# Layer 2's first two weight blocks: the fourth quarter added by VectorE from a second load instead of by an accumulating DMA

## The chip, the cores and the metric

The kernel runs on one core of one Trainium2 chip. The metric is the device time of one execution in microseconds. Before the change it is 2123.89 us, the median of 3 runs (2120.89 to 2127.05). A profile of one more execution shows what each engine did: PE (matmuls), DVE (VectorE), ACT (ScalarE), POOL (GpSimd, here above all an issuer of DMAs) and SP (issues DMAs only).

## The reference

A two-layer encoder on 512 tokens of width 2048: a gated attention layer, then a gated retention layer, each followed by a residual layer norm. The change lies in the first product of the second layer:

```python
def retention_mixer(h, w_in, decay_exp, w_out, cos, sin):
    B, S, _ = h.shape
    proj = h @ w_in                     # 512 x 2048 times 2048 x 12288, float32
    q, k, v, g = jnp.split(proj, [R_QK_WIDTH, 2 * R_QK_WIDTH, 2 * R_QK_WIDTH + R_V_WIDTH], axis=-1)
    ...
    return (o * jax.nn.silu(g)) @ w_out
```

## The kernel before, in words

**Seven products for eight.** The columns of `w_in` are taken 1024 at a time, as twelve *blocks* (`r_in`, numbered from 0). A block is 2048 x 1024 and is cut into four quarters, B11, B12, B21 and B22, of 1024 x 512. The activations are cut likewise. Instead of eight quarter products the kernel makes seven, numbered 1 to 7, each of a *form* of the activations (a sum or difference of their quarters) and a sum of weight quarters. What each product needs of the weights, in the order of a block: 1 takes B11; 2 takes B21; 5 takes B11+B12; 6 takes B11+B12+B22; 3 takes B22; 7 takes B22+B12; 4 takes all four summed.

**Chunks.** A quarter comes as four *chunks* a to d of 128 x 1024 numbers (512 KB). 1/5b below is block 1, product 5, chunk b. Each chunk is split for PE into a high part `whi` (ACT casts it) and a low part `wlo` (DVE subtracts), both at L116, called hi and lo below. PE then makes 12 matmuls of it, three for each of four pairs (L263 with hi, L264 with lo, L265 with hi again), so the first matmul of a chunk needs its hi and the second its lo. There are three buffers for hi and three for lo: a chunk's hi can be written when PE is through with the chunk three before it.

**Order of the products.** PE's order is written by hand. For layer 2's first three blocks it interleaves them (`LAYER_SEQ`): 0/1, 0/2, 1/1, 1/2, 0/5, 0/6, 0/3, 0/7, 1/5, 0/4, 1/6, 1/3, 1/7, 2/1, 1/4, then the rest of block 2. Splits are made two chunks ahead of PE (`AHEAD`), loads are asked for three chunks ahead of a split (`FETCH`). The order on ACT, DVE, POOL and SP is made by a scheduler when the kernel is built; on each engine instructions run strictly in that order, so one that waits holds all behind it.

**Buffers and sums of weights.** Loads (`raw_load`, L126 and L127, from SP) go into the pool `rp`, 9 buffers of a chunk each, or, with `large`, into the pool `xp`, 32 buffers of the same size that hold the activations' quarters and forms. In blocks 0 and 1 (`first`) B11 is loaded again for product 5 and B12 is added to it by an accumulating DMA (`onto`, L144, issued by POOL). That buffer, `v`, then lives through the whole block: B22 is added to it by DVE for product 6 (L182), and when product 6 is split, POOL adds B21 onto it by DMA for product 4 (L203 and L204). B22 has four `rp` buffers of its own from product 6 to 7, and B12 is added onto them by DMA for product 7. In later blocks product 2 comes last but one, so its B21 still lies in SBUF and DVE adds it for product 4 (L183 and L184).

Of the kernel before, what the change touches and what calls it, by code (L numbers as in the profile page):

```python
# [29 lines left out]
R_G = R_HEADS // 2 * 3  # L30
# [22 lines left out]
def encoder_trunk_kernel(  # L53
# [19 lines left out]
    nc = tc.nc  # L73
# [13 lines left out]
    def nm(s):  # L87
        n_names[0] += 1
        return f"{s}{n_names[0]}"
# [4 lines left out]
    def x4(name, dt=F32R):  # L94
        return xp.tile([P, 1024], dt, tag="x", name=nm(name))
# [29 lines left out]
    def raw_load(src, large=False):  # L125
        raw = x4("raw", F32) if large else rp.tile([P, CH], F32, tag="raw", name=nm("raw"))  # L126
        x = nc.sync.dma_start(out=raw, in_=src)  # L127
        if fetched[0] < 12:
            in_turn(x)
        return raw  # L130

    def in_turn(x):

        tc.keep_in_program_order(x)
# [3 lines left out]
    def behind_split(x, n):  # L138

        tc.add_manual_dep(x.ins, los[-n].ins.name, mybir.DependencyInfo(  # L140
            mybir.DependencyClass.NoSync, mybir.DependencyReason.DATA), reason="behind_split")

    def onto(x, src):
        return nc.gpsimd.dma_start(out=x, in_=src, accum_op=ALU.add)  # L144

    class Block:


        def __init__(self, w, first, nc=4, hold=False):

            self.w, self.first, self.nc, self.hold = w, first, nc, hold
            self.got, self.keep, self.bk, self.hooks = {}, {}, {}, {}

        def add(self, seq):
# [7 lines left out]
        def fetch(self, p, c):  # L162
            q = lambda n: self.quarter(n, c)
            g = self.got
            if p == 1:
                g[1 if self.first else "v", c] = raw_load(q(11), self.hold)
            elif p == 2:
                g[2, c] = raw_load(q(21))
            elif p == 6:
                g[3, c] = raw_load(q(22))  # L170
            elif p == 5 and self.first:
                if self.hold:
                    g["v", c] = g[1, c]
                else:
                    g["v", c] = raw_load(q(11))
                    onto(g["v", c], q(12))

        def make(self, p, c):

            g, v = self.got, self.got.get(("v", c))  # L180
            if p == 6:
                nc.vector.tensor_add(v, v, g[3, c])  # L182
            elif p == 4 and not self.first:  # L183
                x = nc.vector.tensor_add(v, v, g[2, c])  # L184
                if self.nc == 4:
                    behind_split(x, 3)
            if p in (3, 7):
                return g[3, c]
            return g[p, c] if p == 2 or p == 1 and self.first else v
# [6 lines left out]
        def follow(self, p, c):  # L196
            q = lambda n: self.quarter(n, c)
            g = self.got
            if p == 1 and not self.first:
                onto(g["v", c], q(12))  # L200
            elif p == 3:
                onto(g[3, c], q(12))
            elif p == 6 and self.first:  # L203
                onto(g["v", c], q(21))  # L204

    class Plain:
# [310 lines left out]


    a_in = [Block(a["wa_in"][g], g < 2, hold=g == 0) for g in range(A_G)]
    r_in = [Block(a["wr_in"][g], g < 2) for g in range(R_G)]  # L520
    a_out = [Plain(a["wa_o"][g], A_KEEP if g == GROUPS - 1 else 4) for g in range(GROUPS)]
    r_pairs = [[Block(a["wr_p"][i, cg], False, 2) for cg in range(2)] for i in range(PAIRS)]
    r_out = [Plain(a["wr_o"][h], 4 - h * (4 - R_KEEP)) for h in range(2)]
# [696 lines left out]
```

## Time and profile before

| | |
|---|---|
| three timed runs | 2127.05, 2123.89, 2120.89 us |
| profiled execution, device time | 2125.48 us |
| its span, first to last instruction | 2123.4 us |
| granted PE clock, mean | 0.997 |
| PE, DVE, ACT, POOL busy | 2102.1, 1602.7, 1102.6, 368.0 us |
| PE waits for other engines, all | 10.4 us |

A row of a timeline gives the start and the duration in us from the span's start, the engine, the line, the operation, what is written and read, and in brackets the idle time of the engine just before, with what ended it. `raw<-raw,raw` at L182 is DVE's addition of B22, `wlo<-raw,whi` the lo of a chunk, `f<-xf,f` the lo of a form of the activations. A row of the windows gives, for a stretch, its length, the busy time of PE, of PE's weight loads, of DVE, ACT and POOL, each with a count, then the granted PE clock, the busy share of the DMA engines and GB/s.

### The profile page before, as it was taken

What the parts mean: (1) busy time and instruction counts of PE and PEld (TensorE: products, weight loads), DVE (VectorE), ACT (ScalarE), POOL (GpSimd) and SP (SyncE); (2) the same over time, 40 slices, a digit from 0 to 9 for tenths busy, and PEclk for the clock granted to TensorE, in tenths of its full rate; (3) what the DMA queues carried; (4) which work ended last, traced back from release to release, by engine and by line L of the source; (5) the groups of instructions that cost most, each with busy time, mean ns of one, the idle gap of its engine ahead of it and who ended that gap; (6) DMA issues with size and microseconds to landing.
All of it is one profiled execution on the core that took longest, in us unless ns stands there. A gap on an engine that the chain in (4) does not pass through costs nothing.

```text
span 2123.4 us, 26496 instructions
## 1 busy us (share of the span) xinstructions
PE 2102.1 (99%) x9756; PEld 1743.3 (82%) x9756; DVE 1602.7 (75%) x2198; ACT 1102.6 (52%) x1457; POOL 368.0 (17%) x453
## 2 busy tenths in 40 slices
PE   9999999999999999999999999999999999999997
PEld 7788888888888887888888888888888878888886
DVE  7778887977677886666877686666686887979767
ACT  6455556655543564454445444444456665656432
POOL 1242322000000112121111111111211122222200
PEclk9999999999999999999999999999999999999999
DMA  9866656563223587686686785576575578877862
GB/s 346 207 143 147 193 152 173 151 224 104 95 70 109 191 186 182 169 226 166 182 234 166 193 219 147 130 209 167 123 211 158 184 180 192 178 192 176 212 199 79
DMA packets 115057, 369.81 MB, mean 174 GB/s; under 512 B 14064, under 2 KB 17136, under 8 KB 114928
## 3 DMA queue, kind: packets, MB, share of 16 engines
q0 software_dynamic: 45568, 148.92, 33.8%
q1 hardware_dynamic: 68928, 218.29, 30.7%
q8 instruction: 76, 1.25, 0.2%
q10 hardware_dynamic: 432, 0.92, 0.1%
q14 instruction: 53, 0.43, 0.1%
HBM read 307.26 MB, written 60.82 MB: 173 GB/s over the span
## 4 chain that ended last, share of the span: by engine, by line
PE 88%; DVE 5%; DMA 4%; issue 2%; POOL 1%; ACT 0%; POOLq 0%; SPq 0%; DVEq 0%; ACTq 0%
PE acc L265 25%; PE acc L264 25%; PE acc L263 25%; PE tr L515 3%; PE o L263 2%; PE o L265 2%; PE o L264 2%; DMA raw<-in_wa_in_dram 1%; DVE wlo L116 1%; PE s L263 1%; PE s L265 1%; PE s L264 1%; DMA xf<-in_xq_dram 1%; DMA q<-qD 1%; DMA raw<-in_wr_p_dram 0%
## 5 line engine op out<-in xcount | busy, mean ns | idle before, releaser
L116 DVE TENSOR_TENSOR wlo<-raw,whi 128x1024 fp32r<-128x1024 f32 (+1 forms) x598 | 727.0, 1217 | 360.0 <-ACT whi L116 354.6
L116 ACT CAST whi<-raw 128x1024 fp32r<-128x1024 f32 (+1 forms) x598 | 626.0, 1050 | 656.9 <-PE acc L265 519.1
L263 PE MATMUL acc<-whi,f 128*128 128x512 f32 x2240 | 881.1, 393 | 3.1 <-ACT whi L116 3.1
L264 PE MATMUL acc<-wlo,f 128*128 128x512 f32 x2240 | 874.2, 390 | 4.0 <-DVE wlo L116 4.0
L265 PE MATMUL acc<-whi,f 128*128 128x512 f32 x2240 | 874.2, 390 | 0.0
L264 PEld LDWEIGHTS acc<-wlo,f 128*128 128x128 f32 x2240 | 421.7, 188 | 91.8 <-DVE wlo L116 6.6
L263 PEld LDWEIGHTS acc<-whi,f 128*128 128x128 f32 x2240 | 421.4, 188 | 89.0 <-ACT whi L116 4.2
L265 PEld LDWEIGHTS acc<-whi,f 128*128 128x128 f32 x2240 | 421.3, 188 | 88.6
L144 POOL DMA_DIRECT2D raw<-in_wr_in_dram x104 | 91.5, 880 | 389.8 <-DVE wlo L116 213.2
L263 PE MATMUL acc<-whi,ogh 128*128 128x512 f32 x288 | 115.6, 401 | 0.4 <-ACT ogh L116 0.4
L265 PE MATMUL acc<-whi,ogl 128*128 128x512 f32 x288 | 112.7, 391 | 0.0
L264 PE MATMUL acc<-wlo,ogh 128*128 128x512 f32 x288 | 112.5, 391 | 0.0
L182 DVE TENSOR_TENSOR raw<-raw,raw 128x1024 f32<-128x1024 f32 x80 | 97.5, 1220 | 8.8 <-DMA raw<-in_wr_in_dram 7.3
L379 ACT COPY t<-acc 128x512 f32<-128x512 f32 x138 | 78.7, 587 | 44.7 <-PE acc L265 40.4
L498 POOL TENSOR_TENSOR rstd<-rs_e,neg_half 128x1 f32<-128x1 f32 x40 | 30.4, 760 | 364.0 <-DVE rs_e L497 363.0
L184 DVE TENSOR_TENSOR raw<-raw,raw 128x1024 f32<-128x1024 f32 x64 | 77.7, 1214 | 0.0
L744 ACT ACTIVATE p<-s,nmax,q_rs 128x512 f32<-128x512 f32 x64 | 49.9, 779 | 33.1 <-DVE nmax L742 26.4
L116 DVE TENSOR_TENSOR f<-xf,f 128x1024 fp32r<-128x1024 f32 (+2 forms) x52 | 59.9, 1155 | 7.7 <-ACT f L116 7.6
L144 POOL DMA_DIRECT2D raw<-in_wa_in_dram x48 | 42.7, 890 | 126.1 <-DVE wlo L116 93.5
L265 PEld LDWEIGHTS acc<-whi,ogl 128*128 128x128 f32 x288 | 54.1, 188 | 12.1 <-DVE ogl L116 0.4
L263 PEld LDWEIGHTS acc<-whi,ogh 128*128 128x128 f32 x288 | 54.2, 188 | 10.2 <-ACT ogh L116 0.8
L264 PEld LDWEIGHTS acc<-wlo,ogh 128*128 128x128 f32 x288 | 54.3, 189 | 9.5
(183 smaller groups left out, 2365.2 us busy)
## 6 DMA issues: line engine op xcount, KB each, us to landing
raw<-in_wr_in_dram SPq DMA_DIRECT2D x152, 512.0 KB, 4.8
raw<-in_wr_in_dram POOLq DMA_DIRECT2D x104, 512.0 KB, 5.9
raw<-in_wa_in_dram SPq DMA_DIRECT2D x62, 512.0 KB, 5.5
raw<-in_wa_in_dram POOLq DMA_DIRECT2D x48, 512.0 KB, 8.4
raw<-in_wr_p_dram SPq DMA_DIRECT2D x36, 512.0 KB, 5.1
raw<-in_wa_o_dram SPq DMA_DIRECT2D x32, 512.0 KB, 3.6
raw<-in_wr_p_dram POOLq DMA_DIRECT2D x24, 512.0 KB, 7.2
yD<-t POOLq DMA_DIRECT2D x36, 256.0 KB, 7.2
```

What stands on the lines that cost most here:

```text
L116: x, y = nc.scalar.copy(hi, src), nc.vector.tensor_sub(lo, src, hi.bitcast(F32))
L144: return nc.gpsimd.dma_start(out=x, in_=src, accum_op=ALU.add)
L182: nc.vector.tensor_add(v, v, g[3, c])
L184: x = nc.vector.tensor_add(v, v, g[2, c])
L263: nc.tensor.matmul(ps, sh, mh, start=start, stop=False, skip_group_check=go_on)
L264: nc.tensor.matmul(ps, sh, ml, start=False, stop=False, skip_group_check=go_on)
L265: nc.tensor.matmul(ps, sl, mh, start=False, stop=stop, skip_group_check=go_on)
L379: nc.scalar.copy(keep[p, t], bk[CHAIN[p]][t])
L498: nc.gpsimd.tensor_tensor(out=dst, in0=e[:, :n], in1=neg_half[:, :n], op=ALU.pow)
L515: nc.tensor.transpose(out=b[:, tcols(i)], in_=src[:, tcols(i)], identity=ident)
L744: nc.scalar.activation(pt, sb, AF.Exp, scale=rs, bias=nmax, accum_out=self.sm[:, h:h + 1])
```

## The change

For layer 2's blocks 0 and 1 (`again`), the accumulating DMA of B21 after product 6 is left out. Instead B21 is loaded once more, from SP into `rp`, when product 4 is due, and DVE adds it to `v` before product 4's split; that addition may not be ordered before the lo of three chunks earlier (`behind_split`). For block 1 (`wide`) B22 comes into `xp` instead of `rp`.

```diff
@@ def fetch(self, p, c):
             elif p == 2:
                 g[2, c] = raw_load(q(21))
             elif p == 6:
-                g[3, c] = raw_load(q(22))
+                g[3, c] = raw_load(q(22), self.wide)
+            elif p == 4 and self.again:
+                g[2, c] = raw_load(q(21))
@@ def make(self, p, c):
-            elif p == 4 and not self.first:
+            elif p == 4 and (not self.first or self.again):
                 x = nc.vector.tensor_add(v, v, g[2, c])
                 if self.nc == 4:
                     behind_split(x, 3)
@@ def follow(self, p, c):
-            elif p == 6 and self.first:
+            elif p == 6 and self.first and not self.again:
                 onto(g["v", c], q(21))
@@
-    r_in = [Block(a["wr_in"][g], g < 2) for g in range(R_G)]
+    r_in = [Block(a["wr_in"][g], g < 2, again=g < 2, wide=g == 1) for g in range(R_G)]
```

Lines behind these are 3 lower in the new kernel (L182 becomes L185, L184 becomes L187). The order of PE's matmuls is the same in both. On SP, the order of the loads from product 1/5 on was, before:

```order
L127 DMA raw1398_7135<-in_wr_in_dram 128x1024
L127 DMA raw1401_7158<-in_wr_in_dram 128x1024
L127 DMA raw1406_7181<-in_wr_in_dram 128x1024
L127 DMA raw1409_7200<-in_wr_in_dram 128x1024
L127 DMA raw1424_7293<-in_wr_in_dram 128x1024
L127 DMA raw1429_7315<-in_wr_in_dram 128x1024
L127 DMA raw1432_7333<-in_wr_in_dram 128x1024
L127 DMA raw1435_7351<-in_wr_in_dram 128x1024
L127 DMA raw1468_7553<-in_wr_in_dram 128x1024
```

raw1398, raw1401, raw1406 and raw1409 are `v` of block 1, chunks a to d; raw1424 to raw1435 are its B22; raw1468 is B11 of 2/1a. Now the same stretch is:

```order
L127 DMA raw1398_7131<-in_wr_in_dram 128x1024
L127 DMA raw1428_7298<-in_wr_in_dram 128x1024
L127 DMA raw1433_7321<-in_wr_in_dram 128x1024
L127 DMA raw1436_7340<-in_wr_in_dram 128x1024
L127 DMA raw1439_7359<-in_wr_in_dram 128x1024
L127 DMA raw1401_7154<-in_wr_in_dram 128x1024
L127 DMA raw1406_7177<-in_wr_in_dram 128x1024
L127 DMA raw1409_7196<-in_wr_in_dram 128x1024
L127 DMA raw1414_7219<-in_wr_in_dram 128x1024
L127 DMA raw1419_7243<-in_wr_in_dram 128x1024
L127 DMA raw1422_7261<-in_wr_in_dram 128x1024
L127 DMA raw1425_7279<-in_wr_in_dram 128x1024
```

B22 of block 1 (raw1428 to raw1439, in `xp`) has moved ahead of three of its `v` chunks, and the second load of block 0's B21 (raw1414 to raw1425, in `rp`) follows them. By the buffers that the scheduler gave them, the load of 0/4a takes that which the lo of 0/7d frees, as B22's first load did before; that of 0/4b takes the buffer which the addition of 0/4a frees, that of 0/4c the one from the addition of 0/4b, and that of 0/4d the one from the lo of 0/4a. The first B22 loads wait for the last splits of the activations' forms 7 and 4.

On DVE, the order from the lo of 1/5a on (not shown) was, before:

```order
L182 TENSOR_TENSOR raw1398_7135<-raw1398_7135,raw1424_7293 128x1024
L116 TENSOR_TENSOR wlo1415_7224<-raw1401_7158,whi1414_7223 128x1024
L386 TENSOR_TENSOR t1376_6997<-t1376_6997,acc1268_6480 128x512
L386 TENSOR_TENSOR t1377_6999<-t1377_6999,acc1269_6481 128x512
L116 TENSOR_TENSOR wlo1419_7246<-raw1406_7181,whi1418_7245 128x1024
L116 TENSOR_TENSOR wlo1421_7262<-raw1409_7200,whi1420_7261 128x1024
L116 TENSOR_TENSOR wlo1423_7278<-raw1334_6794,whi1422_7277 128x1024
L116 TENSOR_TENSOR wlo1426_7296<-raw1343_6824,whi1425_7295 128x1024
```

raw1334, raw1343, raw1346 and raw1351 are `v` of block 0, so the last two rows are the lo of 0/4a and 0/4b. Now:

```order
L185 TENSOR_TENSOR raw1398_7131<-raw1398_7131,raw1428_7298 128x1024
L116 TENSOR_TENSOR wlo1416_7222<-raw1401_7154,whi1415_7221 128x1024
L389 TENSOR_TENSOR t1376_6995<-t1376_6995,acc1268_6480 128x512
L389 TENSOR_TENSOR t1377_6997<-t1377_6997,acc1269_6481 128x512
L187 TENSOR_TENSOR raw1334_6794<-raw1334_6794,raw1414_7219 128x1024
L116 TENSOR_TENSOR wlo1421_7246<-raw1406_7177,whi1420_7245 128x1024
L185 TENSOR_TENSOR raw1401_7154<-raw1401_7154,raw1433_7321 128x1024
L116 TENSOR_TENSOR wlo1424_7264<-raw1409_7196,whi1423_7263 128x1024
L185 TENSOR_TENSOR raw1406_7177<-raw1406_7177,raw1436_7340 128x1024
L187 TENSOR_TENSOR raw1343_6824<-raw1343_6824,raw1419_7243 128x1024
L116 TENSOR_TENSOR wlo1427_7283<-raw1334_6794,whi1426_7282 128x1024
L185 TENSOR_TENSOR raw1409_7196<-raw1409_7196,raw1439_7359 128x1024
```

The additions of B21 (L187) and of B22 (L185) now stand between the lo's of 1/5b to 0/4a. On this go the lo of 0/4b, the additions of 0/4c and 0/4d one after the other, and then the lo of 0/4c.

In block 1's product 4 DVE's order had no additions (wlo1501 and wlo1503 are the lo of 1/4a and 1/4b, the rows ahead those of 2/1b to 2/1d):

```order
L116 TENSOR_TENSOR wlo1489_7663<-raw1473_7585,whi1488_7662 128x1024
L386 TENSOR_TENSOR t1427_7311<-t1427_7311,acc1315_6703 128x512
L386 TENSOR_TENSOR t1428_7313<-t1428_7313,acc1316_6704 128x512
L116 TENSOR_TENSOR wlo1495_7696<-raw1478_7609,whi1494_7695 128x1024
L116 TENSOR_TENSOR wlo1497_7715<-raw1483_7637,whi1496_7714 128x1024
L116 TENSOR_TENSOR wlo1501_7740<-raw1398_7135,whi1500_7739 128x1024
L116 TENSOR_TENSOR wlo1503_7756<-raw1401_7158,whi1502_7755 128x1024
```

Now the four additions stand among them:

```order
L116 TENSOR_TENSOR wlo1494_7669<-raw1477_7589,whi1493_7668 128x1024
L187 TENSOR_TENSOR raw1398_7131<-raw1398_7131,raw1492_7666 128x1024
L389 TENSOR_TENSOR t1431_7317<-t1431_7317,acc1315_6703 128x512
L389 TENSOR_TENSOR t1432_7319<-t1432_7319,acc1316_6704 128x512
L116 TENSOR_TENSOR wlo1501_7704<-raw1482_7613,whi1500_7703 128x1024
L187 TENSOR_TENSOR raw1401_7154<-raw1401_7154,raw1499_7701 128x1024
L116 TENSOR_TENSOR wlo1504_7725<-raw1487_7641,whi1503_7724 128x1024
L116 TENSOR_TENSOR wlo1509_7753<-raw1398_7131,whi1508_7752 128x1024
L187 TENSOR_TENSOR raw1406_7177<-raw1406_7177,raw1502_7722 128x1024
L116 TENSOR_TENSOR wlo1511_7770<-raw1401_7154,whi1510_7769 128x1024
```

The load of 1/4b takes the buffer that the addition of 1/4a frees, and that of 1/4c the one from the addition of 1/4b; that of 1/4d waits on SP behind it.

More of the change, by code (lines that the diff above doesn't have):

```diff
@@ L146, in encoder_trunk_kernel, with __init__ @@
     class Block:
-        def __init__(self, w, first, nc=4, hold=False):
-            self.w, self.first, self.nc, self.hold = w, first, nc, hold
+        def __init__(self, w, first, nc=4, hold=False, again=False, wide=False):
+            self.w, self.first, self.nc, self.hold, self.again, self.wide = w, first, nc, hold, again, wide
             self.got, self.keep, self.bk, self.hooks = {}, {}, {}, {}
```

## The prediction

> **What bounds the kernel now.** I read the page first, then who waited for whom on PE, then the timelines of PE, DVE and ACT around the one wait that lies in layer 2's first blocks. Notation: 1/5b is block 1, product 5, chunk b; "hi" and "lo" are the two halves that ACT and DVE make of a chunk.
>
> ```profile
> span 2123.4 us, 26496 instructions
> PE 2102.1 (99%) x9756; PEld 1743.3 (82%) x9756; DVE 1602.7 (75%) x2198; ACT 1102.6 (52%) x1457; POOL 368.0 (17%) x453
> ```
>
> PE is busy for 2102.1 of 2123.4 us. The order of its matmuls is written by hand and is the same in both kernels, so only its idle time and its clock can change. The idle time with its causes, for the whole run, and then for 800 to 850 us alone (the row after the dots):
>
> ```profile
> PE acc L264 <- DVE wlo L116: 4.0, 5, 1.9
> PE acc L263 <- ACT whi L116: 3.1, 2, 2.2
> PE idle L596 <- DVE two L832: 1.5, 1, 1.5
> PE tr L515 <- ACT p L744: 1.4, 1, 1.4
> PE acc L263 <- ACT ogh L116: 0.4, 1, 0.4
> ...
> PE acc L264 <- DVE wlo L116: 1.9, 1, 1.9
> ```
>
> All waits together are 10.4 us, and the stretch that the change touches (from the removed accumulations, 766.80 us, to block 1's product 4, after 876.88 us) has one of them, of 1.9 us. What it costs in full is read from PE's timeline (start, duration) and from the granted clock in two 5 us windows (the column after the five engines):
>
> ```profile
> 801.90 0.39 PE L263 MATMUL acc<-whi,f 128*128 128x512 f32 x1
> 804.62 0.39 PE L263 MATMUL acc<-whi,f 128*128 128x512 f32 x1
> 806.93 0.50 PE L264 MATMUL acc<-wlo,f 128*128 128x512 f32 x1 [1.92 <-DVE wlo L116]
> 808.72 0.63 PE L264 MATMUL acc<-wlo,f 128*128 128x512 f32 x1
> 813.92 0.39 PE L263 MATMUL acc<-whi,f 128*128 128x512 f32 x1
> ...
> 805.00:810.00 5.00, 3.08 (x11) 2.43 (x10) 4.41 (x6) 2.10 (x2) 1.13 (x2) 0.81 0.74 176
> 810.00:815.00 5.00, 5.00 (x20) 4.09 (x19) 2.24 (x2) 1.93 (x2) 0.00 (x0) 0.85 0.20 55
> ```
>
> 801.90, 804.62 and 813.92 are the first matmuls of 1/5a, 1/5b and 1/5d. A chunk without a wait takes 804.62 - 801.90 = 2.72 us (12 matmuls). From 1/5b to 1/5d are two chunks, 5.44 us, but it took 9.30: **the wait costs 3.86 us**. Of that 2.08 is the gap (806.93 - 804.62 less 0.23), the rest the slow matmuls after it (0.63 us at 808.72) under a clock of 0.81 and 0.85. A shorter wait elsewhere cost only itself: after 1.41 us of idling the next matmuls have 0.39 us again.
>
> ```profile
> 447.46 0.66 PE L515 MATMUL tr<-ident,p 128*128 128x128 f32 x4 [1.41 <-ACT p L744]
> 448.41 0.39 PE L265 MATMUL acc<-whi,ogl 128*128 128x512 f32 x1
> ```
>
> By the Trainium skill (TensorE: Matmul & The Clock Gate, "HAM oscillation — how this bites in real kernels") the clock falls only after idle gaps of more than about 3.4 us. By that rule the wait would have cost 2.1 us; the granted clock of 0.81 behind a gap of 2.3 us says otherwise here, and the measured 3.86 goes into the sum.
>
> Why DVE was late, from its own timeline (idle time and what ended it in brackets) and the chain that ended last:
>
> ```profile
> 795.02 1.23 DVE L116 TENSOR_TENSOR wlo<-raw,whi 128x1024 fp32r<-128x1024 f32 x1 [1.49 <-ACT whi L116]
> 797.74 1.22 DVE L116 TENSOR_TENSOR wlo<-raw,whi 128x1024 fp32r<-128x1024 f32 x1 [1.49 <-ACT whi L116]
> 804.51 1.22 DVE L182 TENSOR_TENSOR raw<-raw,raw 128x1024 f32<-128x1024 f32 x1 [5.55 <-DMA raw<-in_wr_in_dram]
> 805.66 1.22 DVE L116 TENSOR_TENSOR wlo<-raw,whi 128x1024 fp32r<-128x1024 f32 x1
> 806.79 1.28 DVE L386 TENSOR_TENSOR t<-t,acc 128x512 f32<-128x512 f32 x2
> 807.99 1.22 DVE L116 TENSOR_TENSOR wlo<-raw,whi 128x1024 fp32r<-128x1024 f32 x1
> ...
> 796.28 8.14 DMA raw<-in_wr_in_dram
> ```
>
> By the order of DVE the row at 804.51 is the addition of 1/6a, block 1's B22. It stands ahead of the lo of 1/5b (805.66), and waited 5.55 us for its load, which could start only at 796.28, when the lo of 0/7d (795.02 + 1.23) returned a `rp` buffer, and took 8.14 us. The hi of 1/5b had been there since 801.82 (first row):
>
> ```profile
> 800.77 1.05 ACT L116 CAST whi<-raw 128x1024 fp32r<-128x1024 f32 x1 [3.06 <-DMA raw<-in_wr_in_dram]
> 806.23 1.05 ACT L116 CAST whi<-raw 128x1024 fp32r<-128x1024 f32 x1 [4.41 <-DMA raw<-in_wr_in_dram]
> 808.71 1.05 ACT L116 CAST whi<-raw 128x1024 fp32r<-128x1024 f32 x1 [1.43 <-DMA raw<-in_wr_in_dram]
> ```
>
> **Part 1: B22 of block 1 into `xp`.** Removes the late load. The buffers it takes held layer 2's transposed input and come free with the last splits of forms 7 and 4, of which these rows are the first and the last pair (the third row is SP's next load now, that of 1/5b):
>
> ```profile
> 775.43 1.22 DVE L116 TENSOR_TENSOR f<-xf,f 128x1024 fp32r<-128x1024 f32 x1
> 779.98 2.48 DVE L116 TENSOR_TENSOR f<-xf,f 128x1024 fp32r<-128x1024 f32 x2
> ...
> 788.12 0.33 SPq L127 DMA_DIRECT2D raw<-in_wr_in_dram  x1
> ```
>
> So the four loads go out between 776.7 and 782.5, over 13 us before 1/6a is added. SP has nothing else to issue until 788.1, so being put ahead of 1/5b's load costs nothing. The wait of 1.92 us goes: the addition of 1/6a follows the lo of 1/5a at 798.97 and ends at about 800.1, the lo of 1/5b follows its hi (801.82) and ends at 803.1, and PE needs it at 804.85.
>
> **Part 2: the accumulations of B21 go.** Eight POOL issues of about 0.86 us with their transfers, the first and the last of the eight:
>
> ```profile
> 766.80 0.85 POOL L144 DMA_DIRECT2D raw<-in_wr_in_dram  x1 [6.88 <-DVE wlo L116]
> 833.35 0.86 POOL L144 DMA_DIRECT2D raw<-in_wr_in_dram  x1 [1.46 <-DVE m L921]
> ```
>
> POOL is 17% busy, so this gains nothing by itself. Behind the first four on POOL stand the accumulations of product 7, which wait for their own lo splits, and PE did not wait there. Freed DMA time is partly filled by part 1's four loads. I take 0, between 0.5 us earlier and 0.5 us later for the accumulations of 1/5b to 1/5d.
>
> **Part 3: B21 is loaded again and added by DVE.** Eight loads on SP and eight additions. An addition is 1.22 us, 1.14 us where DVE runs on without a pause (805.66 less 804.51). Eight are 9.8 us of DVE. Where DVE idles between splits PE hides them; but they stand ahead of other chunks' lo in DVE's order, and with nine `rp` buffers each load waits until an earlier addition or split returns one. So price each place.
>
> *Block 0's product 4.* The load of 0/4a takes the very slot that 1/6a had: issued 796.28, landed 804.42. DVE: two subtractions after 1/5b's lo to 804.3, addition of 0/4a 804.5 to 805.7, lo of 1/5c after its hi (806.23 + 1.05) 807.3 to 808.5. PE needs that lo at 807.34 + 0.23 = 807.57: wait 0.95. Next on DVE: 1/6b to 809.6, lo of 1/5d (hi ready 809.76) to 811.0, in time; 1/6c to 812.1; 0/4b, whose load left at 805.7 and had 6 us, to 813.25; lo of 0/4a to 814.4, needed at 811.02 + 2.72 + 0.23 = 813.97: wait 0.45. Then 1/6d and the lo of 0/4b to 816.7, in time. The loads of 0/4c and 0/4d leave at 813.25 and 814.4. How long they take, and two others of its kind, from three stretches of L127 (786:812, 812:826, 858:880):
>
> ```profile
> DMA to landing us min/median/max: 3.4/5.1/8.1
> ...
> DMA to landing us min/median/max: 3.3/3.6/3.7
> ...
> DMA to landing us min/median/max: 4.3/5.7/7.6
> ```
>
> At that time the DMA engines are half idle (second stretch), so 3.6 us: landed at 816.9 and 818.1, added to 819.4, lo of 0/4c to 820.6, needed at 819.85: wait 0.75. Together **2.15 us** in three waits, each under the 1.41 us that left the clock alone. Bounds: 0, if the accumulations land 1 us sooner; 10 us, if the loads of 0/4b to 0/4d each take the 8.1 us of the first stretch (waits of 0.95, 2.35 and 3.4 us, the last two with 1.7 us of slow clock each).
>
> *Block 1's product 4.* No PE wait stands here now. The rows are DVE's lo of 2/1b and two needed times of PE:
>
> ```profile
> 860.18 1.23 DVE L116 TENSOR_TENSOR wlo<-raw,whi 128x1024 fp32r<-128x1024 f32 x1 [1.45 <-ACT whi L116]
> ...
> 871.42 0.39 PE L264 MATMUL acc<-wlo,f 128*128 128x512 f32 x1
> 876.88 0.39 PE L264 MATMUL acc<-wlo,f 128*128 128x512 f32 x1
> ```
>
> 1/4a is added at 861.4 to 862.5; only then its buffer is free for the load of 1/4b. With a landing time of L, 1/4b is added by 863.8 + L, the lo of 2/1d queued behind it is ready at 864.9 + L (needed 871.42), the load of 1/4c leaves at 863.8 + L, and the lo of 1/4b behind its addition is ready at 866.2 + 2L (needed 876.88). It holds up to L = 5.3. The third stretch's median is 5.7: **0.8 us**. Bounds 0 and, at its slowest 7.6 us, 1.1 + 3.4 + 1.7 of slow clock = 6.2.
>
> **Sum:** 3.86 goes, 2.15 + 0.8 come: -0.9 us. The profiled execution took 2125.48 us (span 2123.4), 1.6 above the median of 2123.89; -0.9 from the median gives **2123.0**. What a measurement of this kernel can tell is about 0.3%, 6.4 us, and nothing that is removed is as large.
>
> **The rivals.** *All waits vanish* (the accumulations land sooner because four of them are gone, and L stays under 5.3): -3.86, 2120.0. For it: freed DMA time; against it: DVE runs without a pause from 804.5 to 814. Chance 0.2.
>
> *Slower: the new loads become a chain.* Each waits for the addition of the one before, so a late load is paid again by the next. It decides at L = 5.3 us in block 1's product 4, and each us above costs 2. At 7.6 us: 2.15 + 6.2 - 3.86 = +4.5, 2128.4; with the 8.1 us in block 0 as well, 10.1 + 6.2 - 3.86 = +12.4, 2136.3. For it: the DMA engines are nearly full from 859 to 880 (share 0.95, row below), against it: 0.46 in block 0's place.
>
> ```profile
> 809.00:826.00 17.00, 17.00 (x71) 13.90 (x71) 11.05 (x10) 8.10 (x9) 0.00 (x0) 0.93 0.46 154
> 859.00:880.00 21.00, 21.00 (x100) 17.43 (x99) 9.95 (x9) 10.31 (x13) 6.95 (x9) 1.00 0.95 246
> ```
>
> Chance 0.15, a third of it above 0.3%. *It doesn't do what it says:* the `xp` buffers come free too late and 1/6a still holds DVE: 2123.9, chance 0.05; the splits at 775 to 782 speak against it. *Short gaps leave the clock alone*, so the old wait was worth only 2.08: 2.95 - 2.08 = +0.9, 2124.8; chance 0.05. This is the rule of the Trainium skill's page above, and the row at 808.72 speaks against it.
>
> **How the numbers follow.** The forecast, several short waits for one long, has 0.55. The range reaches from the first rival less 1.5 us, since single runs of before lie 6 us apart (2120.89 to 2127.05), to the lower price of the slower one: 2118.5 to 2128.5. It leaves out the upper price. All but the upper end of the slower rival lie within 0.3% of 2123.89: same 0.91. Slower 0.05. Faster 0.04, for what I have not seen: no case reaches 2117.5.
>
> **What would show it.** Right: no DVE wait for a DMA at L185 before the lo of 1/5b; PE waits of under 1 us at about 808, 814 and 820 us; granted clock 1.00 around 805; loads of L127 at 776 to 783. Wrong: a PE wait of over 2 us between 800 and 885, or a second stretch of slow clock, or no wait at all.

## The result, and the profile after

| | before | after |
|---|---|---|
| median of 8 runs | 2123.72 us | 2130.17 us |
| lowest to highest | 2120.89 to 2127.05 | 2126.79 to 2133.39 |
| the profiled execution, its span | 2125.48, 2123.4 | 2129.43, 2127.7 |

The ratio is 1.0033, with a 95% interval of 1.0024 to 1.0042: slower by 0.33%, or 7.0 us (5.1 to 8.9). The forecast of 2123.0 us is 7 us off, and the median lies 1.7 us above the end of the range.

Lines of the kernel after stand three numbers further down than before from L182 on: L185 and L187 are the additions for products 6 and 4, L266 to L268 the three matmuls, L267 the one that reads lo. The page of after:

```profile
span 2127.7 us, 26511 instructions
PE 2102.9 (99%) x9756; PEld 1739.9 (82%) x9756; DVE 1611.7 (76%) x2206; ACT 1102.6 (52%) x1457; POOL 363.6 (17%) x445
```

PE is busy as long as before, to 0.8 us: the time came as waits. PE's waits (us in all, times, the longest) in the whole run, then from 795 to 826 us, then from 868 to 890 us:

```profile
PE acc L267 <- DVE wlo L116: 9.1, 12, 2.1
PE acc L266 <- ACT whi L116: 1.9, 2, 1.3
...
PE acc L267 <- DVE wlo L116: 2.9, 4, 1.4
PE acc L266 <- ACT whi L116: 1.3, 1, 1.3
...
PE acc L267 <- DVE wlo L116: 4.0, 3, 2.1
```

So there are two places. To count all that is lost in a stretch I take the first matmuls of two chunks and subtract what lies between them where nothing waits. From 0/6a to 2/5a it took 115.56 us before (769.26 to 884.82) and 122.72 after (766.72 to 889.44). Less the 3.86 of its one wait, the kernel before gives 111.70 us without waits: 3.86 and 11.02 lost, and the difference of 7.16 agrees with the measured slowdown. (The two profiled executions are only 4.3 us apart in span, above all because this one of before reached 0/6a 2.5 us later.) Cut at 1/6a, the first place lost 6.07 us (before 3.86) and the second 4.95 (before 0). That is more than the waits listed, 4.2 and 4.0 us: they are counted from a matmul's end, which is 0.16 us after the next one starts when nothing waits, and the first matmul behind a wait takes 0.50 us instead of 0.39.

**The first place.** ACT's casts of 0/7a to 0/7d before (those of 1/5b to 1/5d stand in the prediction), then those of 0/7a to 1/5c after, where the row at 794.78 is 0/7d and 1/5a (start, duration, what ended ACT's idling):

```profile
785.78 1.05 ACT L116 CAST whi<-raw 128x1024 fp32r<-128x1024 f32 x1 [1.67 <-PE acc L265]
788.50 1.05 ACT L116 CAST whi<-raw 128x1024 fp32r<-128x1024 f32 x1 [1.67 <-PE acc L265]
791.22 1.06 ACT L116 CAST whi<-raw 128x1024 fp32r<-128x1024 f32 x1 [1.67 <-PE acc L265]
793.94 1.05 ACT L116 CAST whi<-raw 128x1024 fp32r<-128x1024 f32 x1 [1.66 <-PE acc L265]
```

```profile
783.24 1.06 ACT L116 CAST whi<-raw 128x1024 fp32r<-128x1024 f32 x1 [1.66 <-PE acc L268]
787.13 1.05 ACT L116 CAST whi<-raw 128x1024 fp32r<-128x1024 f32 x1 [2.83 <-DMA raw<-in_wr_in_dram]
790.89 1.05 ACT L116 CAST whi<-raw 128x1024 fp32r<-128x1024 f32 x1 [2.71 <-DMA raw<-in_wr_in_dram]
794.78 2.00 ACT L116 CAST whi<-raw 128x1024 fp32r<-128x1024 f32 x2 [2.84 <-DMA raw<-in_wr_in_dram]
801.10 1.05 ACT L116 CAST whi<-raw 128x1024 fp32r<-128x1024 f32 x1 [4.32 <-DMA raw<-in_wr_in_dram]
806.46 1.04 ACT L116 CAST whi<-raw 128x1024 fp32r<-128x1024 f32 x1 [4.30 <-DMA raw<-in_wr_in_dram]
```

Before, each cast waited for PE to give back a buffer: the weights were early. After, from 0/7b on, each waits for a DMA: 0/7b to 0/7d for the accumulations of product 7, 1/5b and 1/5c for those of product 5. How long product 7's four accumulations took (L144, issues between 778 and 787 us before, 770 and 785 after):

```profile
DMA to landing us min/median/max: 5.9/6.9/7.6
...
DMA to landing us min/median/max: 7.5/9.1/11.3
```

What they met is in the DMA share (the column ahead of the last, which is GB/s) of 766 to 774 us and 774 to 795 us, before and then after:

```profile
766.00:774.00 8.00, 8.00 (x37) 6.62 (x36) 8.00 (x8) 5.04 (x6) 2.12 (x3) 1.00 0.67 104
774.00:795.00 21.00, 21.00 (x94) 17.40 (x93) 15.74 (x15) 12.41 (x14) 5.23 (x7) 1.00 1.02 214
```

```profile
766.00:774.00 8.00, 8.00 (x37) 6.60 (x37) 8.00 (x8) 5.72 (x7) 0.00 (x0) 1.00 0.00 0
774.00:795.00 21.00, 21.00 (x94) 17.41 (x93) 13.22 (x13) 9.82 (x12) 3.44 (x4) 1.00 0.95 249
```

The engines were full from 774 us on before the change too (the share adds up packet times, so it can pass 1). After, they stand still until 774, because product 7's first accumulation leaves only at 775.62 and the wide loads can't start before the last splits return their buffers. Counted from 0/6a's first matmul, 774.27 after is 776.81 before, and by then about 1.2 of the 2.1 MB that the change frees, B21's four accumulations, had moved (115 GB/s from 766 to 776.8 us): the wide loads can't use that part. Then four loads of 512 KB and the accumulations go out together (the wide loads, L127 from 770 to 785 us):

```profile
L127 SPq DMA_DIRECT2D raw<-in_wr_in_dram x4: 327/328/328, 774.3 to 780.0; - x4
DMA to landing us min/median/max: 3.6/8.2/11.5
```

**The second place** is the chain of the slower rival. DVE from 860 us on (L187 is an addition of block 1's product 4), and PE's longest wait:

```profile
860.99 1.22 DVE L187 TENSOR_TENSOR raw<-raw,raw 128x1024 f32<-128x1024 f32 x1
...
869.93 1.23 DVE L187 TENSOR_TENSOR raw<-raw,raw 128x1024 f32<-128x1024 f32 x1 [5.38 <-DMA raw<-in_wr_in_dram]
871.07 2.36 DVE L116 TENSOR_TENSOR wlo<-raw,whi 128x1024 fp32r<-128x1024 f32 x2
876.51 1.23 DVE L187 TENSOR_TENSOR raw<-raw,raw 128x1024 f32<-128x1024 f32 x1 [3.09 <-DMA raw<-in_wr_in_dram]
877.66 1.22 DVE L116 TENSOR_TENSOR wlo<-raw,whi 128x1024 fp32r<-128x1024 f32 x1
881.66 1.22 DVE L187 TENSOR_TENSOR raw<-raw,raw 128x1024 f32<-128x1024 f32 x1 [2.78 <-DMA raw<-in_wr_in_dram]
882.80 1.22 DVE L116 TENSOR_TENSOR wlo<-raw,whi 128x1024 fp32r<-128x1024 f32 x1
...
884.07 0.50 PE L267 MATMUL acc<-wlo,f 128*128 128x512 f32 x1 [2.09 <-DVE wlo L116]
```

The load of 1/4b left when 1/4a's addition returned its buffer (862.24) and took 7.7 us, that of 1/4c (871.18) took 5.3, that of 1/4d (873.45) 8.2. The los of 2/1d, 1/4b and 1/4c stand behind the additions of 1/4b, 1/4c and 1/4d, and PE waits for each: counted like the first place, 1.4, 1.2 and 2.4 us are lost.

### The profile page after: what moved, and what is told of

Read it like the earlier page. It is cut to its first block, busy times and chain, and to the rows that moved or that the text cites. A ratio compares the mean times of both kernels' runs of the same rounds, so it can differ in the third digit from the quotient of the medians.

```text
span 2127.7 us, 26511 instructions
## 1 busy us (share of the span) xinstructions
PE 2102.9 (99%) x9756; PEld 1739.9 (82%) x9756; DVE 1611.7 (76%) x2206; ACT 1102.6 (52%) x1457; POOL 363.6 (17%) x445
## 4 chain that ended last, share of the span: by engine, by line
PE 83%; issue 8%; DMA 4%; DVE 3%; POOL 1%; ACT 0%; POOLq 0%; SPq 0%; DVEq 0%; ACTq 0%
PE acc L267 23%; PE acc L268 23%; PE acc L266 23%; PE tr L518 3%; PE o L266 2%; PE o L268 2%; PE o L267 2%; PE s L266 1%; PE s L268 1%; PE s L267 1%; DMA raw<-in_wr_in_dram 1%; DMA raw<-in_wa_in_dram 1%; DVE wlo L116 1%; DMA xf<-in_xq_dram 1%; POOL raw L144 1%
## 5 line engine op out<-in xcount | busy, mean ns | idle before, releaser
L267 PE MATMUL acc<-wlo,f 128*128 128x512 f32 x2240 | 874.5, 390 | 9.3 <-DVE wlo L116 9.1
L266 PE MATMUL acc<-whi,f 128*128 128x512 f32 x2240 | 880.0, 393 | 1.9 <-ACT whi L116 1.9
L268 PE MATMUL acc<-whi,f 128*128 128x512 f32 x2240 | 873.2, 390 | 0.0
L267 PEld LDWEIGHTS acc<-wlo,f 128*128 128x128 f32 x2240 | 420.8, 188 | 101.6 <-DVE wlo L116 17.0
L266 PEld LDWEIGHTS acc<-whi,f 128*128 128x128 f32 x2240 | 420.7, 188 | 88.0 <-ACT whi L116 3.2
L268 PEld LDWEIGHTS acc<-whi,f 128*128 128x128 f32 x2240 | 420.5, 188 | 87.9
L144 POOL DMA_DIRECT2D raw<-in_wr_in_dram x96 | 84.7, 888 | 407.7 <-DVE wlo L116 216.8
L266 PE MATMUL acc<-whi,ogh 128*128 128x512 f32 x288 | 115.6, 402 | 0.4 <-ACT ogh L116 0.4
L268 PE MATMUL acc<-whi,ogl 128*128 128x512 f32 x288 | 112.7, 391 | 0.0
L267 PE MATMUL acc<-wlo,ogh 128*128 128x512 f32 x288 | 112.5, 391 | 0.0
L185 DVE TENSOR_TENSOR raw<-raw,raw 128x1024 f32<-128x1024 f32 x80 | 97.6, 1222 | 1.4
L187 DVE TENSOR_TENSOR raw<-raw,raw 128x1024 f32<-128x1024 f32 x72 | 87.7, 1218 | 12.5 <-DMA raw<-in_wr_in_dram 12.5
L268 PEld LDWEIGHTS acc<-whi,ogl 128*128 128x128 f32 x288 | 54.0, 188 | 12.2 <-DVE ogl L116 0.4
L144 POOL DMA_DIRECT2D raw<-in_wa_in_dram x48 | 42.5, 886 | 123.6 <-DVE wlo L116 91.5
L266 PEld LDWEIGHTS acc<-whi,ogh 128*128 128x128 f32 x288 | 54.2, 188 | 10.2 <-ACT ogh L116 0.8
L267 PEld LDWEIGHTS acc<-wlo,ogh 128*128 128x128 f32 x288 | 54.3, 189 | 9.5
```

Of the source, the lines that this page charges most:

```text
L266: nc.tensor.matmul(ps, sh, mh, start=start, stop=False, skip_group_check=go_on)
L267: nc.tensor.matmul(ps, sh, ml, start=False, stop=False, skip_group_check=go_on)
L268: nc.tensor.matmul(ps, sl, mh, start=False, stop=stop, skip_group_check=go_on)
```

## The experiments

Two theories went in. **A**: the wide loads take time on the DMA engines from product 7's accumulations, and the second loads of B21 form a chain. **B**: the wide loads cost nothing; the additions on VectorE and the nine buffers make both losses. The time of each kernel is given as its ratio to the kernel before, run on the same chip in the same rounds; 0.1% is 2.1 us. "Lost" is counted as above, from one profile each, first place and second.

### The parts of the change

e1, only the wide loads:

```
-    r_in = [Block(..., g < 2, again=g < 2, wide=g == 1) ...]
+    r_in = [Block(..., g < 2, wide=g == 1) ...]
```

> Only block 1's B22 comes into the large buffers; B21 is accumulated by POOL as in the kernel before. Theory A (the wide loads crowd the DMA queues: product 7's accumulations land later, and that is part of the 6.1 us that the changed kernel loses between 795 and 825 us): the old wait goes (-3.9 us), but waits of 1 to 3 us for a lo or hi come at 1/5a to 1/5c; 1 to 3 us under before. Theory B (the wide loads cost nothing, the eight additions on VectorE alone make both losses): no PE wait between 790 and 885 us and 3.9 us under before.

Measured: ratio 1.0020 (1.0010 to 1.0030), 4.2 us; lost 5.41 and 0. That the wide loads cost nothing, theory B's first half, is refuted: with none of the additions for product 4, PE waits at 0/7c, 0/7d, 1/5b and 1/5c. Theory A's cause holds, but its size was too small: it said 1 to 3 us under before.

e2, block 0's B21 again and the wide loads (`again=g == 0, wide=g == 1`):

> As the changed kernel, but block 1's B21 is accumulated by POOL as before; block 0's B21 is loaded again. Theory A and B alike: the waits at 2/1d and at block 1's product 4 (4.95 us) are gone, those between 795 and 825 us (6.1 us) stay: -3.9 + 6.1 = 2.2 us over before, 4.9 under the changed kernel. Rival C (the places are not apart: a later start of one moves the other): more than 2 us away from that.

Measured: 1.0024 (1.0015 to 1.0032), 5.1 us; lost 5.52 and 0. The second place is gone and the first keeps its size, so by the profile the places are apart. The time does not show it: it is 2.9 us over the 2.2 expected, which was to speak for rival C.

e3, block 1's B21 again and the wide loads (`again=g == 1, wide=g == 1`):

> As the changed kernel, but block 0's B21 is accumulated by POOL as before; block 1's B21 is loaded again. Theory A: block 1's product 4 still loses 4.95 us, 1/5 loses the 1 to 3 us of the wide loads: 2 to 4 us over before. Theory B: 4.95 - 3.9 = 1 us over before, with no PE wait between 790 and 860 us.

Measured: 1.0042 (1.0029 to 1.0054), 8.9 us; lost 8.55 (with one stretch of half clock) and 4.58. Against e1 the second place comes back, and the time is 4.7 us more. But in this profile the first place lost 3.1 us more than in e1 as well, 1.7 of it by the half clock. The expected 2 to 4 us over before was too small.

e4, both blocks again, no wide loads (`again=g < 2`):

> B21 is loaded again in blocks 0 and 1, but block 1's B22 stays in the nine small buffers, so its four loads stand behind the four of 0/4. Theory A: without the wide loads product 7's accumulations land as before (1/5a and 1/5b without a wait), but 0/4 and 1/6 are one chain of eight loads, each waiting for a buffer: waits of 6 to 12 us in all between 805 and 835 us, and 4.95 us at block 1's product 4: 7 to 13 us over before. Theory B: the order on VectorE is all that counts, 1/6's additions come after 0/4's, so 4 to 6 us there and 4.95: 5 to 7 us over before, hardly above the changed kernel.

Measured: 1.0028 (1.0019 to 1.0038), 5.9 us; lost 3.53 and 5.29. Product 7's four accumulations, issued from 778.1 to 785.8 us as before the change, landed sooner than before:

```profile
DMA to landing us min/median/max: 5.4/5.6/6.3
```

This is the gain of the accumulations that the change removes: 6.9 to 5.6 us. The wide loads take it from 5.6 to 9.1. The size fell within B's numbers here (A's chain of 6 to 12 us between 805 and 835 did not come); the landing is A's.

### Taking the suspects away

e6, the changed kernel without the transfer of block 1's B22, its buffers filled by ScalarE, so that the product leaves B22 out:

```
-                g[3, c] = raw_load(q(22), self.wide)
+                if self.wide:
+                    g[3, c] = x4("raw", F32)
+                    nc.scalar.copy(g[3, c]..., ident...broadcast_to([P, 8, P]))
+                else:
+                    g[3, c] = raw_load(q(22))
```

> The changed kernel without the four wide loads: ScalarE fills block 1's large buffers from a constant instead (block 1's B22 is left out). VectorE's order is that of the changed kernel. Theory A (the wide loads delay product 7's accumulations): these land as they did before the change, measured from the matmuls; 1/5b's load takes about 6 us instead of 9.3; of the 6.1 us lost between 795 and 825 us some 2 to 3 are left, so 3 to 4 us under the changed kernel. Theory B (the additions on VectorE and the nine buffers make that loss): it stays at 5 to 6 us and the time is that of the changed kernel.

Measured: 1.0025 (1.0016 to 1.0035), 5.3 us; lost 3.95 and 2.88. 0/7d's accumulation lands 23.3 us after the first matmul of 0/6a, where the changed kernel has 28.0 and the kernel before 24.1: the delay is the wide loads'. But of the 6.07 us only 2.1 go with it; the rest are waits at 1/5b, 1/5c, 0/4a and, longest with 1.6 us, 0/4c. Theory A expected 3 to 4 us of it, and theory B's second half, that additions and buffers cost much of the first place, holds. The second place lost 2.1 us less too: the loads of 1/4b and 1/4d took 6.3 and 7.4 us there instead of 7.7 and 8.2.

e7, block 1's second B21 in large buffers:

```
             elif p == 4 and self.again:
-                g[2, c] = raw_load(q(21))
+                g[2, c] = raw_load(q(21), self.wide)
```

> The changed kernel with block 1's second loads of B21 in large buffers too, so that none waits for an addition. Theory A: the waits at 2/1d and at block 1's product 4 (4.95 us) go, the first place keeps its 6.1 us: 5 us under the changed kernel, 1 to 3 us over before. Rival (the DMA engines are full there whatever the buffers): at least half of the 4.95 us stays, now at 2/1 or 2/5.

Measured: 1.0018 (1.0009 to 1.0026), 3.8 us; lost 5.42 (with one stretch of half clock) and 0. The chain is what costs in the second place; the time is 3.2 us under the changed kernel, where 5 were expected. SyncE issues the four loads with others between 817.0 and 858.3 us, and the additions find their data there (L127 in that stretch, and DVE's additions at L187):

```profile
L127 SPq DMA_DIRECT2D raw<-in_wr_in_dram x11: 327/328/328, 817.0 to 858.3; - x11
DMA to landing us min/median/max: 3.4/4.7/5.6
```

```profile
864.09 1.22 DVE L187 TENSOR_TENSOR raw<-raw,raw 128x1024 f32<-128x1024 f32 x1
867.56 1.22 DVE L187 TENSOR_TENSOR raw<-raw,raw 128x1024 f32<-128x1024 f32 x1
870.01 1.22 DVE L187 TENSOR_TENSOR raw<-raw,raw 128x1024 f32<-128x1024 f32 x1
873.27 1.22 DVE L187 TENSOR_TENSOR raw<-raw,raw 128x1024 f32<-128x1024 f32 x1
```

e8, all eight second loads in large buffers (`raw_load(q(21), True)`):

> The changed kernel with all eight second loads of B21 in large buffers. SyncE now issues block 0's four in the place of block 1's B22, ahead of 1/5b's load, and B22 after 1/5d. Theory A: four loads of 512 KB at 774 to 780 us delay product 7's accumulations just as B22's did, and B22's then fall among the accumulations of 1/5: the waits up to 1/5c stay (4 us or more), only those of 0/4 and block 1's product 4 go: 0 to 3 us over before. Theory B (buffers and chains are all): no wait over 0.5 us between 790 and 890 us, 3 to 4 us under before.

Measured: 1.0014 (1.0005 to 1.0022), 3.0 us; lost 5.95 and 0; all listed waits lie up to 1/5c, and 5.1 us of the loss. SyncE puts 0/4's four loads at 775 to 781 us, and 0/7d's accumulation lands at 28.4 us, as with B22's in their place. It is the transfer at that time that counts, whichever quarter it brings.

### What the old wait was worth

e5, the kernel before with the additions of block 1's B22 behind the los of 0/4 (`late` is set for block 1 alone):

```
             if p == 6:
-                nc.vector.tensor_add(v, v, g[3, c])
+                x = nc.vector.tensor_add(v, v, g[3, c])
+                if self.late:
+                    behind_split(x, 4)
```

> The kernel before with one edit: the additions of block 1's B22 stand behind the los of 0/4 in VectorE's order; no load moves, B21 is accumulated as before. If the old wait is VectorE's order and nothing else, the lo of 1/5b follows its hi, the wait of 2.1 us and the slow clock behind it go, and 0.95 us of waiting for 1/5c stays (its accumulation lands at 806.1 us): 2.9 us under before. Rival: 1/5's accumulations are what PE then waits for, one after the other: less than 1.5 us under before.

Measured: 0.9994 (0.9985 to 1.0003); lost 3.76 and 0. The wait behind the addition is gone, and PE loses as much to the accumulations of 1/5b and 1/5c, which land 3.1 and 2.6 us later than before (34.5 and 39.5 us after 0/6a's first matmul, before 31.4 and 36.9). The time is the rival's. From 790 to 826 us:

```profile
PE acc L266 <- DVE wlo L116: 1.5, 2, 0.8
PE acc L265 <- ACT whi L116: 1.1, 2, 0.9
```

e9, the same with two stores of block 0's product 3 moved behind 1/5's accumulations on POOL:

```
+        elif nb == 1 and blk is r_in[0] and t < 2:
+            soon(8, lambda: behind_split(nc.gpsimd.dma_start(out=vD2[...][:, t], in_=src), 3))
```

> The kernel of the late additions (e5), with block 0's two stores of product 3 (256 KB each) moved on POOL from ahead of 1/5c's accumulation to behind those of 1/5 and product 7's stores. If the stretch from 795 to 811 us is bound by what lands there, the accumulations of 1/5b and 1/5c land 1.5 to 3 us sooner, the 3.8 us that PE still lost at 1/5b and 1/5c shrink to 1 to 2, and the time is 3 to 4.5 us under before (ratio 0.998 to 0.9985). If PE's loss there has another cause: the time of the late additions, 0 to 2 us under before.

Measured: 0.9987 (0.9978 to 0.9996), median 2120.87 us, 2.8 us under before: this beats both kernels, though only a little. Lost 0.32 and 0, and from 790 to 826 us the profile lists no PE wait at all. The expected mechanism is shown only in part: the accumulations of 1/5b and 1/5c land 2.7 and 3.5 us sooner than in e5, counted from 0/6a's first matmul (31.8 and 36.0 us), but 0/7d's, which is ahead of the moved stores, is 2.9 us sooner already. Against the kernel before, 1/5c lands 0.9 us sooner.

e10, the kernel before once more; e11, the wide loads only once more; e12, e5 once more, with its time:

> The kernel before, unchanged, profiled a second time, for how far landings differ between executions of one program. In the first profile 0/7d's accumulation landed 24.1 us after the first matmul of 0/6a, in the late additions' 26.4, though both programs are the same up to there. If landings repeat, 24.1 again within 0.3 us; if they differ by execution, anywhere between 23.5 and 27 us.

> The kernel with the wide loads only (e1), profiled a second time: its first profile was the fastest of 12 executions, 6 us under their median, and lost 5.4 us between 795 and 825 us with no slow clock. If the median's extra time lies in that stretch, this profile shows 8 to 11 us lost there or slow clock behind the waits; if it lies elsewhere, 5 to 6 us again and the rest in other waits.

> The late additions (e5) once more. In e5's profile 0/7d's accumulation landed 26.4 us after the first matmul of 0/6a, against 24.1, 24.0 and 23.5 in three other executions of a program that is the same up to there, and PE lost 3.8 us at 1/5b and 1/5c. If that execution was an outlier: 23.5 to 24.1 us here, 0.9 to 1.2 us lost, at 1/5c alone, and 2 to 3 us under before. If the late additions themselves bring the later landing: 26 us and 3.5 to 4 us lost again, and 0 to 1.5 us under before.

Measured: e10 lost 3.95, and 0/7d's accumulation landed at 24.0 us: landings repeat. e11 lost 6.01, at 30.2 us (e1 29.6), and took 2125.26 us in its one execution: neither the 8 to 11 us nor a slow clock that would have explained e1's median. e12 lost 3.65, at 25.8 us (e5 26.4), with a ratio of 0.9999 (0.9989 to 1.0009). So e5 was no outlier: both executions of this kernel land late, though the order up to there is that of the kernel before. The late additions alone don't bring it, since e9 has them too and lands at 23.5. Why is open.

| kernel | 0/7d lands, us after 0/6a | lost, first + second | ratio |
|---|---|---|---|
| before (e10) | 24.1 (24.0) | 3.86 + 0 (3.95 + 0) | 1 |
| after | 28.0 | 6.07 + 4.95 | 1.0033 |
| e1 wide only (e11) | 29.6 (30.2) | 5.41 + 0 (6.01 + 0) | 1.0020 |
| e2 block 0 again, wide | 27.9 | 5.52 + 0 | 1.0024 |
| e3 block 1 again, wide | 29.5 | 8.55 + 4.58 | 1.0042 |
| e4 both again, not wide | 22.9 | 3.53 + 5.29 | 1.0028 |
| e5 late additions (e12) | 26.4 (25.8) | 3.76 + 0 (3.65 + 0) | 0.9994 (0.9999) |
| e6 no B22 transfer | 23.3 | 3.95 + 2.88 | 1.0025 |
| e7 block 1's B21 large | 27.9 | 5.42 + 0 | 1.0018 |
| e8 all B21 large | 28.4 | 5.95 + 0 | 1.0014 |
| e9 late additions, late stores | 23.5 | 0.32 + 0 | 0.9987 |

The landing falls into groups: 23 to 24 us without four loads ahead of it, 28 with them, 29.5 to 30 with them and B21's accumulations as well; only e5 stands between. The loss against before agrees with the measured time for after, e3, e4, e5, e8 and e9 within the intervals; e1, e2, e6 and e7 measure about 2 to 3.5 us more than their profiles lose (e1: 1.6 to 2.2 in the profiles, 4.2 in time). In e2 and e7 about half of that rest can be clock: the mean granted clock of their executions is 0.9966 where that of before is 0.9974, by an estimate (0.0008 of 2123 us) some 1.6 us. In e1 and e6 it is nearer (0.9973 and 0.9971), and the rest stays open.

## Why the prediction was wrong

**What bounds the kernel** was right: PE's busy time and the order of its matmuls are unchanged, and all 7 us are lost in the stretch that was named. The sum gave -0.9 us there, and 7.2 came. Of the 8.1 us between them 4.15 lie in block 1's product 4 (4.95 for 0.8) and 3.9 in the first place (6.07 for 2.15); of these 2.1 go with the wide loads.

**Part 1, that the wide loads cost nothing, failed**, and it is the step to learn from, since it was put at nothing. It priced them on SP's queue, where nothing else waited, and not on the DMA engines, which all queues share. The price stood in the DMA queue rows of the kernel before, which the sum did not use. From 766 to 812 us (packets, MB, share of the 16 engines; q0 carries POOL's transfers, q1 SP's four loads):

```profile
q0 software_dynamic: 1904, 6.82, 76.2%
q1 hardware_dynamic: 576, 2.10, 12.2%
```

Four plain loads take 12.2% of 46 us, 5.6 us of all engines; and q0, accumulations but for four stores of 256 KB, moved 6.82 MB in 76.2%, 35 us, half as fast (195 GB/s against 374). The engines were full from 774 to 795 us (share 1.02), so what is put there comes out as delay: 5.5 us at 0/7d with B21's accumulations still there (29.6 less 24.1). With them gone it is 5.1 (28.0 less 22.9), though without the loads the engines then idle up to product 7's first accumulation (e4: share 0.08 from 774 to 780 us, 0.97 from 780 to 795). That accumulation leaves 8.9 us after 0/6a's first matmul, the four loads at 7.6 to 13.3, so little of them finds idle engines. The Trainium skill says it (DMA: Bandwidth & Descriptors, "Issuing engines are not separate DMA queues"): transfers from different engines run on the same 16 DMA engines and interleave. The trace agrees: loads from SP's queue delayed POOL's accumulations by these 5 us.

**Part 2, "within 0.5 us", failed** for the same reason. Taking B21's accumulations away did gain 1.2 us by itself (24.1 to 22.9 in e4), and no more, since product 7's accumulations leave when their los are done, at the same time as before (778.1 to 785.8 us). Both parts together moved 0/7d's landing by 3.9 us. 1/5b's load left at the same point, 18.9 us after 0/6a's first matmul, and landed 3.4 us later (28.1, before 24.7), so its accumulation landed 2.9 us later (34.3, before 31.4).

**The old wait's 3.86 us** was the cost of a wait, but what its removal alone brings is not settled. In e5 and e12 the wait is gone, 3.7 us are lost at 1/5b and 1/5c instead, and the time doesn't change; but their accumulations land 2.5 to 3.1 us later than in the kernel before, for a reason that stays open. In e9 they land at 31.8 and 36.0 us, and 0.32 us is lost. That goes with the prediction's 0.95 us at 1/5c, which was worked out for a landing at 36.9. What the prediction lacked is that the landings don't stay where they were.

**Part 3, block 0's product 4**, was given 2.15 us and is part of 6.07. Without the wide loads' transfer 3.95 is left (e6), most of it at 1/5c, 0/4a and 0/4c, the places that were named. So the step's own error is about 1.8 us, and part 1's 2.1 come on top. The largest piece is 0/4c, given 0.75 us: 1.9 in e6 and 1.7 after. Its lo stands behind the addition of 0/4d, whose load took 4.7 us after (814.68 to 819.41) where 3.6 was taken.

**Part 3, block 1's product 4**, was given 0.8 us and cost 4.95: the largest error, and it has two parts. L = 5.7 was too small. It was the median of four loads, the first two of which took 7.6 and 6.6 us; the load of 1/4b took 7.7, and in a chain the late one counts (the median of after's five loads there is 5.7 again: 5.3/5.7/8.2). With the measured 7.7 and 5.3 in place of 2L, the formula gives 2.3 us up to 1/4b; 2.55 were lost there. The other 2.4 us were lost at 1/4c, which the formula doesn't have: its lo stands behind the addition of 1/4d. From the same rows, as an estimate, 1/4d's load leaves when the los of 2/1d and 1/4a are done, at 866.0 + L, and the lo of 1/4c is ready at 868.4 + L + L', where L and L' are the loads of 1/4b and 1/4d; PE needed it at 879.60 before. With 7.7 and 8.2 that is 4.7 us late in all (4.95 measured), with e6's 6.3 and 7.4 it is 2.5 (2.88 measured).

**The slower rival** had the mechanism right, a chain in which late loads are paid again. That its 4.5 us at 7.6 (without slow clock) comes near 4.95 is luck: it took two loads of 7.6 us, where the second took 5.3, and left out the wait at 1/4c. No rival had the wide loads on the DMA engines, and so 0.05 for more than 0.3% was too little. The wait of over 2 us that was named as the sign of being wrong is there: 2.09 us, at 884.07. **The clock**: the half clock behind the old wait is gone as forecast, and the profile after shows none between 6 and 2118 us; for the wait at 884.07 that is luck, as the windows below show.

## What to carry to other kernels

A transfer that is moved, in time or to another buffer, has to be priced on the DMA engines: read their share and the queues' rate in the stretch that it goes to and in the one that it leaves; time freed in one stretch doesn't help a later one. Where each load waits for the buffer of the one before, put a late landing into the sum (here the median was 5.7 us, and the loads that counted took 7.7 and 8.2), or break the chain with buffers of its own (e7: 4.95 us to 0). Then ask of every chunk in the chain, to the last, which lo stands behind its addition: the one that was left out was half of the cost here. And before a wait is counted as a gain, move only its cause and see what PE waits for next (e5).

## What the runs showed of the hardware

**Half clock follows a window, not a gap.** Between the first and the last microseconds of a run, all stretches of half clock are 3.413 us long, but for one of twice that (e12), and those of one execution lie on one grid. In the windows of this grid ahead of them PE was busy (second number) 1.49, 1.58 and 1.50 us of 3.41; before, e7 and e2, each with the window behind it (the granted clock is the third number from the end):

```profile
804.65:808.06 3.41, 1.49 (x7) 0.96 (x6) 3.41 (x5) 1.05 (x1) 0.23 (x1) 1.00 0.92 181
808.06:811.47 3.41, 3.41 (x10) 2.66 (x9) 2.37 (x3) 1.43 (x2) 0.90 (x2) 0.50 0.43 159
```

```profile
809.22:812.63 3.41, 1.58 (x7) 0.75 (x6) 1.82 (x3) 1.32 (x2) 0.06 (x1) 1.00 1.04 268
812.63:816.04 3.41, 3.41 (x10) 2.65 (x9) 3.32 (x4) 1.72 (x2) 0.00 (x0) 0.50 0.47 187
```

```profile
445.73:449.14 3.41, 1.50 (x9) 1.25 (x9) 1.77 (x3) 2.35 (x5) 0.54 (x1) 1.00 1.04 417
449.14:452.55 3.41, 3.41 (x10) 2.56 (x9) 2.48 (x7) 1.34 (x3) 0.00 (x0) 0.50 0.74 291
```

In the kernel after, the gap of 2.1 us at 884.07 fell across two windows, and the clock stayed:

```profile
879.79:883.20 3.41, 2.19 (x10) 1.46 (x8) 1.54 (x2) 0.00 (x0) 0.00 (x0) 1.00 0.90 357
883.20:886.62 3.42, 2.55 (x11) 2.11 (x12) 3.09 (x3) 2.00 (x2) 0.00 (x0) 1.00 0.74 253
```

Over the profiles, windows at full clock with 1.58 us busy or less were always followed by half clock, windows at full clock with 1.79 or more never; between them both occur (1.73 with it in e3 and without it in e5). A window that was itself at half clock is another case: in e12 one with 2.65 us of PE, whose matmuls take longer at half clock, was followed by a second one at half clock. So a wait of about 2 us costs 1.7 us more or nothing, by where it falls: part of the spread between executions, and a reason to trust no single one. Over 94 executions of the kernel before, the median time is 2126.3 us where the mean granted clock was 0.996 (16 of them) and 2121.5 where it was 0.999 (8); one such stretch takes 0.0008 off the mean, by 3.413 us at half clock. The Trainium skill (TensorE: Matmul & The Clock Gate, "What's actually happening") has the free-running window of 3413 ns, and the grid agrees; it lets the clock fall after a window of idleness, and here a window that was about half idle was enough.

**An accumulating DMA runs at about half the rate** of a plain load (195 against 374 GB/s by the queue rows above; four stores are in the 195). **Landings repeat**: one program gave 24.1 and 24.0 us, a second 29.6 and 30.2, a third 26.4 and 25.8, each pair within 0.6 us. So differences of more than 1 us between kernels at such a point mean something even with one profile each.
